# Gate and up products of three batches ahead of the norm's second half, and the down product in seven passes over all chunks

## The chip, the cores and the metric

One core of a Trainium2 chip runs the whole program. The metric is the device time of one execution in microseconds (us), lower is better. Matmuls run on TensorE (PE), elementwise work on VectorE (DVE), ScalarE (ACT) and GpSimd (POOL), and SyncE (SP) issues the DMAs. `sf`, `sr`, `hf`, `hr` are SBUF tiles, `bk` are PSUM banks, `xd`, `yd`, `td` are scratch arrays in DRAM.

## The reference

Two layers over x of 1024 tokens by 1024 features, in float32. The mixer (attention) of either layer is untouched by the change but for its first projection.

```python
for layer in range(2):
    h = rms_norm(x, attn_norm_g[layer])
    x = x + mixer(h)                      # layer 0: even_mixer, layer 1: diff_mixer
    h = rms_norm(x, ffn_norm_g[layer])
    x = x + swiglu(h, w_gate, w_up, w_down)

def swiglu(h, w_gate, w_up, w_down):      # w_gate, w_up: 1024 x 2816, w_down: 2816 x 1024
    a = einsum('bsd,df->bsf', h, w_gate)
    u = einsum('bsd,df->bsf', h, w_up)
    return einsum('bsf,fd->bsd', silu(a) * u, w_down)
```

## The kernel before, in words

Activations lie transposed: features on the 128 partitions, tokens along the free axis, in two token halves `th` = 0 and 1 of 512. Every float32 operand of a product is split in a rounded high part, which ACT casts (L102), and a low part, which DVE subtracts (L1031); a product is then three matmuls: high by high, high by low, low by high. In the gate these are L1138, L1139 and L1140, in the down product L1051, L1052 and L1053, in the output projection L374, L375 and L376.

The feed-forward multiplies by a scheme of seven products for a 2 by 2 block matrix (in place of eight), with sums of blocks made ahead of the products and sums of results behind them. In **gate and up** the left operands are the blocks of w_gate and w_up, loaded for one batch (two column tiles of 128, of eleven such pairs) at a time; the right operands B0 to B6 are the four blocks of the normalised x (rows: halves of the features; columns: halves of the tokens) and three sums of them. Only B0 and B1 are plain blocks of the first token half. One batch is seven products `i` of 2 x 4 x 3 = 24 matmuls, so a layer has 11 x 7 x 24 = 1848. `prep_gate` makes the left operands of a product (POOL sums in `left`, L1060 to L1064, then the split), `gate` runs it and drains the PSUM banks, and `hidden` writes the seven combinations of the hidden activations that the down product wants to `td`.

`out_rest` stands ahead of that: for th = 0 and then th = 1 it ends the output projection, adds the residual (L994), writes y, sums the squares, turns the sum into 1/rms (`rms`: two matmuls with a constant `sub`, L339 and L340, and DVE and ACT steps L334 to L350), and scales each of eight tiles by gain and 1/rms on DVE (L1000). For th = 0 it splits the tiles into B0 and B1; then, with both halves there, it makes the sums for B2 to B6 on DVE and POOL (L1011 to L1020) and splits them. The products stand behind all of it, batch after batch, each batch with i = 0 to 6.

**Down** takes the eleven pairs of chunks in three groups of 4, 4 and 3. Within a group all seven products run, each over the group's pairs: seven steps of 48, 48 or 36 matmuls, 924 a layer. `w_down` is loaded once per group, the right operands are read back from `td`. After each product its four banks are drained; `add_x` then reads a tile of y (residual so far) from DRAM, adds, and writes it back, once per group, and the last group writes x (layer 0) or the output (layer 1). In layer 0 the last group also feeds the next norm: squares and the split of x into the next mixer's operands.

The order of work comes from `stages`, a list of (prepare, run, ahead): `feed_forward` prepares a gate product three steps before it runs and a down product one step before. Inside that, a scheduler sets each engine's order, and pools of tiles (`Slots`) set when a buffer comes free. In layer 0 the first half's `rms` comes three steps before the end of the list and the second half's at its end; after that the next mixer starts with `first_project` (a value projection in 256-wide matmuls, L465 to L467, then L374 to L376), whose weights `w_load` splits on ACT and POOL (L220).

The lines around which the change turns:

```python
GROUPS = [range(0, 4), range(4, 8), range(8, 11)]
DOWN = [0, 1, 2, 3, 6, 4, 5]
...
for b in range(self.BATCHES):
    for i in range(7):
        yield partial(self.prep_gate, b, i), partial(self.gate, b, i), 3
for g in range(len(self.GROUPS)):
    for s in range(7):
        yield partial(self.prep_down, g, s), partial(self.down, g, s), 3 if g == s == 0 else 1
```

Of the kernel before, what the change touches and what calls it, by code (L numbers as in the profile page):

```python
# [18 lines left out]
P = 128  # L19
D = 1024  # L20
S = 1024
KC = 8
# [94 lines left out]
class Trunk:  # L117
# [379 lines left out]
    def first_project(self, st, vs, gains):  # L497
# [5 lines left out]
        for th in range(2):  # L503
            for k in range(KC):
# [297 lines left out]
    def mixer(self, l, gains, window, window_cost, forget=None):  # L802

        st, vs = deque(), deque()
        self.first_project(st, vs, gains(0))
# [163 lines left out]
    def out_rest(self, l):  # L969


        nc = self.nc
        if 6 not in self.loaded:
            self.load_o(l, 6)
        self.sr.put(*self.oH[0:6], *self.oL[0:6])
        w = [self.w_next(), self.w_next()]
        for th in range(2):
            sl = slice(th * TH, th * TH + TH)
            for k in sorted(self.apart):
                nc.sync.dma_start(self.x_tile(k, th), self.p_dram[k][:, sl])  # L980
        Slots.join(self.sr, self.sf)
        Slots.join(self.hr, self.hf, self.raw)
        self.take_raw(0)
        acc = self.sf.get()
        g0 = G_FFN0 if l == 0 else G_FFN1
        for th in range(2):
            sl = slice(th * TH, th * TH + TH)
            for k in range(KC):
                ps = self.rF.get()
                c = slice(k * P, k * P + P)  # L990
                self.mm3(ps[:], [y[2][:, 0, c] for y in w], [y[3][:, 0, c] for y in w],
                         [r32(t[:, sl]) for t in self.oH[6:]], [r32(t[:, sl]) for t in self.oL[6:]])
                x = self.x_at(k, th)
                nc.vector.tensor_tensor(x, ps[:], x, ALU.add)  # L994
                nc.sync.dma_start(self.y_dram[k][:, sl], x)
                self.squares(acc, x, k, k < 2)
            self.rms(acc, th)
            for k in range(KC):
                x = self.x_at(k, th)
                nc.vector.scalar_tensor_tensor(x, x, self.gains[:, g0 + k:g0 + k + 1], self.rt[:, sl],  # L1000
                                               ALU.mult, ALU.mult)
                if th == 0:
                    self.B[k % 2].append(self.split(x))
            if th == 0:
                self.prep_to(2)
        for x in w:
            self.sr.put(x[0], x[1])
        self.sr.put(*self.oH[6:], *self.oL[6:])
        self.sf.put(acc)
        xs = [[self.x_at(2 * j + e, t) for e in range(2) for t in range(2)] for j in range(4)]  # L1010
        for b11, b12, b21, b22 in xs:  # L1011
            nc.vector.tensor_tensor(b11, b12, b11, ALU.subtract)
            nc.gpsimd.tensor_tensor(b12, b22, b12, ALU.subtract)
            self.B[5].append(self.split(b22))
            nc.vector.tensor_tensor(b22, b22, b11, ALU.subtract)
            self.B[2].append(self.split(b22))
            nc.gpsimd.tensor_tensor(b21, b21, b22, ALU.subtract)
        for i, place in ((3, 1), (4, 0), (6, 2)):
            for j in range(4):
                self.B[i].append(self.split(xs[j][place]))  # L1020
                if i != 4:
                    self.sf.put(self.xt[(4 if i == 3 else 0) + j])

    def split(self, x):

        t = self.sr.get()
        h, l = t[:, 0:TH], t[:, TH:2 * TH]
        if len(x.shape) == 3:
            h, l = (y.rearrange("p (j c) -> p j c", j=4) for y in (h, l))
        self.S.copy(r32(h), x)  # L1030
        self.nc.vector.tensor_tensor(r32(l), x, h, ALU.subtract)  # L1031
        return t
# [8 lines left out]


    def products(self, ps, WT, BT, c, first, last):

        nc = self.nc
        n = len(WT)
        for j in range(n):
            w, b = WT[j], BT[j]
            wh, wl = r32(w[:, c]), r32(w[:, TH + c.start:TH + c.stop])
            bh, bl = r32(b[:, 0:TH]), r32(b[:, TH:2 * TH])  # L1050
            nc.tensor.matmul(ps, wh, bh, start=first and j == 0, stop=False, skip_group_check=True)  # L1051
            nc.tensor.matmul(ps, wh, bl, start=False, stop=False, skip_group_check=True)  # L1052
            nc.tensor.matmul(ps, wl, bh, start=False, stop=j == n - 1, skip_group_check=True)  # L1053

    def left(self, i, A, tmp):

        p = self.nc.gpsimd
        a11, a12, a21, a22 = A
        if i == 2:
            p.tensor_tensor(tmp, a21, a22, ALU.add)  # L1060
            p.tensor_tensor(a21, a11, a21, ALU.subtract)
            p.tensor_tensor(a11, tmp, a11, ALU.subtract)
        if i == 5:
            p.tensor_tensor(a12, a12, a11, ALU.subtract)  # L1064
        return self.split((a11, a12, a11, a21, tmp, a12, a22)[i])


    BATCHES = NF // 2

    def take_raw(self, b):  # L1070

        self.raws[b] = []
        for f in (2 * b, 2 * b + 1):
            t = [self.sf.get(), self.sf.get()]
            for x, src in zip(t, (self.a["wg"], self.a["wu"])):
                self.nc.sync.dma_start(x[:].rearrange("p (k c) -> p k c", k=8), src[self.l, f])
            self.raws[b].append(t)

    def prep_gate(self, b, i):
        if i == 1 and b + 1 < self.BATCHES:  # L1080
            self.take_raw(b + 1)
        elif b + 1 == self.BATCHES and i in (1, 4):
            self.take_down(0, 0 if i == 1 else 2)
        out = []
        for n, (g, u) in enumerate(self.raws[b]):
            A = [x[:].rearrange("p (j e c) -> p j e c", j=4, e=2)[:, :, e, :] for x in (g, u) for e in range(2)]
            if i == 2:
                self.tmp[n] = self.hf.get()
            s1 = self.tmp[n][:].rearrange("p (j c) -> p j c", j=4) if self.tmp[n] is not None else None
            out.append(self.left(i, A, s1))  # L1090
            if i == 4:
                self.hf.put(self.tmp[n])
                self.tmp[n] = None
            if i == 6:
                self.sf.put(g, u)
        return out

    def gate(self, b, i, W):
        nc = self.nc
        for n in range(2):  # L1100
# [3 lines left out]
            self.products_gate(ps, W[n], self.B[i], i)  # L1104
            self.sr.put(W[n])
            v = self.v[n]
            if i == 0:
                v["p"], v["s"] = self.hf.get(), self.hf.get()
                self.S.copy(v["p"][:], ps)
            elif i == 1:  # L1110
                self.S.activation(v["s"][:], ps, AF.Silu)
            elif i == 2:
                v["u"] = self.hf.get()
                nc.vector.tensor_tensor(v["u"][:], ps, v["p"][:], ALU.add)
            elif i == 3:
                nc.vector.tensor_tensor(v["p"][:], ps, v["p"][:], ALU.add)
            elif i == 4:
                v["q"] = self.hf.get()
                nc.vector.tensor_tensor(v["q"][:], ps, v["p"][:], ALU.add)
            elif i == 5:  # L1120
                u = v["u"][:]
                nc.vector.tensor_tensor(u, ps, u, ALU.add)
                self.S.activation(u, u, AF.Silu)
                nc.gpsimd.tensor_tensor(u, u, v["q"][:], ALU.mult)
            else:
                nc.vector.tensor_tensor(v["p"][:], ps, v["p"][:], ALU.add)
                nc.gpsimd.tensor_tensor(v["s"][:], v["s"][:], v["p"][:], ALU.mult)
        if b == self.BATCHES - 1:
            self.sr.put(*self.B[i])
        if i == 6:  # L1130
            self.hidden(b)

    def products_gate(self, ps, w, B, i):
        nc = self.nc
        for j in range(4):
            wh, wl = (r32(w[:, o + j * P:o + j * P + P]) for o in (0, TH))
            bh, bl = r32(B[j][:, 0:TH]), r32(B[j][:, TH:2 * TH])
            nc.tensor.matmul(ps, wh, bh, start=i in (0, 2, 4, 6) and j == 0, stop=False, skip_group_check=True)  # L1138
            nc.tensor.matmul(ps, wh, bl, start=False, stop=False, skip_group_check=True)  # L1139
            nc.tensor.matmul(ps, wl, bh, start=False, stop=j == 3, skip_group_check=True)  # L1140

    def hidden(self, b):

        nc = self.nc
        x, y = self.v
# [289 lines left out]
```

## Time and profile before

| | before |
|---|---|
| median of 3 runs | 2727.14 us (2722.53 to 2727.82) |
| the profiled execution: time, span | 2726.96 us, 2725.1 us |
| PE busy | 2482.8 us, 91% of the span |
| DVE, ACT, POOL busy | 1906.0, 1287.8, 958.8 us (70%, 47%, 35%) |
| DMA | 331.64 MB, mean 122 GB/s |
| chain that ended last: PE, DVE, ACT, POOL, DMA | 65%, 15%, 5%, 5%, 5% |

The span is the time from the first to the last recorded work. The busy share is a mean over stages: layer 0's feed-forward runs from about 668 to 1392 us, layer 1's from about 2006 us to the end, and in both the gate's steady part has PE busy throughout. "PEclk" in the rows below is the granted TensorE clock of a stretch, 1.00 being the higher of its two levels (2.4 GHz) and 0.50 the lower (1.2 GHz).

### The profile page before, as it was taken

To read this page: it belongs to the slowest core of one execution; us is meant where nothing else is said; L and a number is where in the kernel's file an instruction comes from. 1 tells how busy PE (TensorE), PEld (TensorE's weight loads), DVE (VectorE), ACT (ScalarE), POOL (GpSimd) and SP (SyncE) were. 2 spreads that over 40 slices of the span, in tenths; PEclk is the share of its full clock that TensorE was granted. 3 is DMA by queue.
4 is the path that set the end of the run, shared out by engine and by line. 5 is a ranking of instruction groups with operands and counts; after the bars stand their busy time and mean duration, and the time that the engine had idled before them with its cause. 6 is when DMAs were issued, how large, how long until landed. Compare 5 with 4: busy or idle time off the path is not lost.

```text
span 2725.1 us, 35163 instructions
## 1 busy us (share of the span) xinstructions
PE 2482.8 (91%) x11896; PEld 2032.0 (75%) x11896; DVE 1906.0 (70%) x3411; ACT 1287.8 (47%) x2598; POOL 958.8 (35%) x760
## 2 busy tenths in 40 slices
PE   8898899998499999998969999998967999998997
PEld 7776778776388888777758877876745888886786
DVE  6869858987865556576756687778677555656775
ACT  5656666754433233434446576666443323333332
POOL 4112111123354444424552232223134444434643
PEclk9999999999699999999989999999988999999998
DMA  5323152463023223466533232235421322345654
GB/s 174 91 57 81 28 125 82 118 208 140 34 94 108 101 105 116 175 222 208 184 130 85 67 98 76 79 90 146 138 93 66 108 101 104 116 145 200 231 182 162
DMA packets 157488, 331.64 MB, mean 122 GB/s; under 512 B 19539, under 2 KB 25460, under 8 KB 157308
## 3 DMA queue, kind: packets, MB, share of 16 engines
q1 hardware_dynamic: 157308, 329.41, 38.2%
q8 instruction: 93, 1.52, 0.2%
q14 instruction: 87, 0.71, 0.1%
HBM read 199.27 MB, written 88.11 MB: 105 GB/s over the span
## 4 chain that ended last, share of the span: by engine, by line
PE 65%; DVE 15%; ACT 5%; POOL 5%; DMA 5%; issue 4%; SPq 1%; POOLq 0%; DVEq 0%; ACTq 0%
PE bk L1139 10%; PE bk L1138 10%; PE bk L1140 10%; PE bk L375 4%; PE bk L376 4%; PE bk L374 4%; PE bk L1051 3%; PE bk L1052 3%; PE bk L1053 3%; PE bk L687 3%; PE bk L565 3%; DVE sf L583 2%; PE bk L673 2%; ACT sf L110 1%; DVE sr L1031 1%
## 5 line engine op out<-in xcount | busy, mean ns | idle before, releaser
L102 ACT CAST sr<-sf 128x512 fp32r<-128x512 f32 (+1 forms) x690 | 409.4, 620 | 777.8 <-PE bk L1140 309.0
L1031 DVE TENSOR_TENSOR sr<-sf,sr 128x512 fp32r<-128x512 f32 x628 | 515.3, 847 | 166.4 <-ACT sr L102 165.1
L1138 PE MATMUL bk<-sr,sr 128*128 128x512 f32 x1232 | 483.7, 394 | 46.7 <-ACT sr L102 45.7
L1139 PE MATMUL bk<-sr,sr 128*128 128x512 f32 x1232 | 483.9, 393 | 45.8 <-DVE sr L1031 45.8
L1140 PE MATMUL bk<-sr,sr 128*128 128x512 f32 x1232 | 481.8, 391 | 0.0
L374 PE MATMUL bk<-sr,sr 128*128 128x512 f32 x768 | 307.0, 400 | 4.9 <-ACT sr L102 2.7
L1138 PEld LDWEIGHTS bk<-sr,sr 128*128 128x128 f32 x1232 | 233.1, 190 | 100.3 <-ACT sr L102 50.0
L375 PE MATMUL bk<-sr,sr 128*128 128x512 f32 x768 | 305.6, 398 | 2.3 <-DVE sr L928 2.3
L1139 PEld LDWEIGHTS bk<-sr,sr 128*128 128x128 f32 x1232 | 233.2, 189 | 98.3 <-DVE sr L1031 50.4
L376 PE MATMUL bk<-sr,sr 128*128 128x512 f32 x768 | 304.0, 396 | 1.2 <-POOL sr L220 1.2
L220 POOL TENSOR_TENSOR sr<-raw,sr 128x512 fp32r<-128x512 f32 (+2 forms) x140 | 189.1, 1365 | 314.8 <-ACT sr L102 181.5
L1051 PE MATMUL bk<-sr,sr 128*128 128x512 f32 x616 | 249.2, 405 | 46.3 <-ACT sf L102 30.8
L1140 PEld LDWEIGHTS bk<-sr,sr 128*128 128x128 f32 x1232 | 233.0, 189 | 48.6 <-DVE sr L1031 0.4
L1052 PE MATMUL bk<-sr,sr 128*128 128x512 f32 x616 | 246.9, 401 | 0.0
L1053 PE MATMUL bk<-sr,sr 128*128 128x512 f32 x616 | 246.2, 400 | 0.0
L565 PE MATMUL bk<-sr,sr 128*128 128x512 f32 (+2 forms) x768 | 200.3, 359 | 9.0 <-ACT sf L110 8.1
L1252 POOL TENSOR_TENSOR hf<-hf,hf 128x512 f32<-128x512 f32 x72 | 106.3, 1485 | 257.5 <-DVE hf L1236 245.7
L687 PE MATMUL bk<-hr,sr 128*128 128x512 f32 (+2 forms) x560 | 165.4, 388 | 14.1 <-DVE hr L705 11.5
L1051 PEld LDWEIGHTS bk<-sr,sr 128*128 128x128 f32 x616 | 120.1, 195 | 77.6 <-ACT sf L102 35.0
L102 ACT CAST hr<-bk 128x512 fp32r<-128x512 f32 (+2 forms) x240 | 122.4, 525 | 104.8 <-PE bk L673 92.3
L705 DVE TENSOR_TENSOR hr<-bk,hr 128x512 fp32r<-128x512 f32 (+2 forms) x240 | 142.4, 604 | 41.4 <-ACT hr L102 39.9
L374 PEld LDWEIGHTS bk<-sr,sr 128*128 128x128 f32 x768 | 145.3, 189 | 33.9 <-ACT sr L102 3.7
(189 smaller groups left out, 4886.3 us busy)
## 6 DMA issues: line engine op xcount, KB each, us to landing
td<-hf SPq DMA_DIRECT2D x154, 256.0 KB, 2.0
sf<-td SPq DMA_DIRECT2D x154, 256.0 KB, 4.2
sr<-sr SPq DMA_DIRECT2D x96, 256.0 KB, 3.5
hf<-yd SPq DMA_DIRECT2D x96, 256.0 KB, 3.9
sf<-in_wg_dram SPq DMA_DIRECT2D x44, 512.0 KB, 3.9
sf<-in_wu_dram SPq DMA_DIRECT2D x44, 512.0 KB, 3.6
sf<-in_wd_dram SPq DMA_DIRECT2D x44, 512.0 KB, 5.8
raw<-in_w_dram SPq DMA_DIRECT2D x64, 256.0 KB, 3.0
```

The lines of the kernel that those rows point to most:

```text
L102: self.last = self.e.copy(out, in_)
L374: nc.tensor.matmul(ps, WH[k], hH[k], start=first and k == 0, stop=False)
L375: nc.tensor.matmul(ps, WH[k], hL[k], start=False, stop=False)
L376: nc.tensor.matmul(ps, WL[k], hH[k], start=False, stop=last and k == n - 1)
L565: nc.tensor.matmul(b[:, 0:hi - lo], r32(Q[i // 4][:, q]), r32(KK[:, lo:hi]), start=j == 0, stop=j == 1)
L1031: self.nc.vector.tensor_tensor(r32(l), x, h, ALU.subtract)
L1051: nc.tensor.matmul(ps, wh, bh, start=first and j == 0, stop=False, skip_group_check=True)
L1052: nc.tensor.matmul(ps, wh, bl, start=False, stop=False, skip_group_check=True)
L1053: nc.tensor.matmul(ps, wl, bh, start=False, stop=j == n - 1, skip_group_check=True)
L1138: nc.tensor.matmul(ps, wh, bh, start=i in (0, 2, 4, 6) and j == 0, stop=False, skip_group_check=True)
L1139: nc.tensor.matmul(ps, wh, bl, start=False, stop=False, skip_group_check=True)
L1140: nc.tensor.matmul(ps, wl, bh, start=False, stop=j == 3, skip_group_check=True)
```

## The change

It reorders the gate and rewrites the down product; the number of matmuls stays.

- **Early products.** i = 0 and 1 of batches 0, 1 and 2 come first (`EARLY = 3`); then i = 2 to 6 of these three; then batches 3 to 10 as before. `out_rest` is called once per token half. The gain is put on by ACT (`scale`), the factor 1/rms by four 1024-wide DVE products (L998). B2 to B6 are made in five parts (`rights_late`), one beside each of the steps 2 to 6, in 1024-wide operations, and their sums run on DVE alone. The results of i = 0 and 1 of batches 1 and 2 wait in an `sf` tile; w_gate of batches 1 and 2 is loaded a second time when its turn comes.
- **Down.** Seven passes, each one product over all eleven pairs: 77 steps of 12 matmuls. Each pass keeps its sums in four PSUM banks, 0 to 3 or 4 to 7 in turn, and they are drained at its end only (`take`). w_down stays in 22 SBUF tiles, loaded as 44 blocks of 256 KB a layer; the block sums (33 and 11 a layer) are made in place on POOL ahead of the passes that want them (`sums`). y is read once for each of the 16 tiles and x written once.
- **Next norm.** In layer 0 `next_norm` is spread over the last twelve steps, four `w_load` of the next mixer come in the last five, and the `rms` of the second token half moves between the halves of `first_project`, by way of a call that `mixer` hands on.

The new lines are L1046 for the low part of a 512-wide split and L1039 for a 1024-wide one, L1102 to L1104 for the gate's matmuls, L1236 to L1238 for the down product's. The diff, cut to its core:

```diff
+    def out_rest(self, l, th, w, acc, gain):
...
+            x = self.x_at(k, th)
+            self.S.activation(x, x, AF.Copy, scale=self.gains[:, gain + k:gain + k + 1])
...
+        for t in self.xt[4 * th:4 * th + 4]:
+            y = t[:].rearrange("p (e c) -> p e c", e=2)
+            nc.vector.tensor_tensor(y, y, r, ALU.mult)
...
+    def rights_late(self):
+
+        v, x = self.nc.vector, self.xt
+        for m in range(2):
+            v.tensor_tensor(x[4 + m][:], x[6 + m][:], x[4 + m][:], ALU.subtract)
+            v.tensor_tensor(x[m][:], x[4 + m][:], x[m][:], ALU.add)
+            self.B[2].append(self.split2(x[m]))
+        yield
...
+    PASSES = [0, 6, 1, 2, 4, 3, 5]
+    BLOCKS = [0, 3, 1, 2]
...
+    def sums(self, s):
+
+        p, n = self.nc.gpsimd, self.PAIRS
+        while self.n3 < n and s >= 2 * n - 2 + self.n3 * 13 // 10:
+            a11, a21, a22 = (self.block(x, self.n3) for x in (0, 2, 3))
+            p.tensor_tensor(a22, a21, a22, ALU.add)
+            p.tensor_tensor(a21, a11, a21, ALU.subtract)
+            p.tensor_tensor(a11, a22, a11, ALU.subtract)
+            self.n3 += 1
...
+    def prep_down(self, s):
+        i, j = self.PASSES[s // self.PAIRS], s % self.PAIRS
+        self.loads(s, s)
+        self.sums(s)
+        W = self.split(self.block((0, 1, 0, 2, 3, 1, 3)[i], j))
+        pool, t = self.rights.popleft()
+        R = self.split(t[:, 0:TH])
...
+        banks = self.bank[0:4] if n % 2 == 0 else self.bank[4:8]
...
+            if j == self.PAIRS - 1:
+                self.take(i, u, ps)
...
+        if i in (0, 6, 4):
+            self.S.copy(at(i), ps)
+        elif i == 2:
+            nc.vector.tensor_tensor(at(2), ps, at(0), ALU.add)
...
+        elif i == 1:
+            t = self.x_old(u, 0)
+            nc.vector.tensor_tensor(t[:], ps, t[:], ALU.add)
...
+        elif i == 3:
+            nc.vector.tensor_tensor(at(0), ps, at(0), ALU.add)
+            for x, th in ((6, 0), (4, 1)):
+                nc.vector.tensor_tensor(at(x), at(x), at(0), ALU.add)
+                self.x_new(u + 4, th, at(x))
...
+        todo = [(b, i) for b in range(self.EARLY) for i in range(2)]
+        todo += [(b, i) for b in range(self.EARLY) for i in range(2, 7)]
+        todo += [(b, i) for b in range(self.EARLY, self.BATCHES) for i in range(7)]
...
+        self.out_rest(l, 0, w, acc, gain)
+        for t in range(4):
+            self.B[t // 2].append(self.split2(self.xt[t]))
+        prep_to(2)
+        self.take_raw(0, (1,))
+        self.out_rest(l, 1, w, acc, gain)
...
+            prep_to(m + (3 if m < 7 * self.EARLY else 4 if s < 0 else 5))
+            run(made[m])
+            made[m] = None
+            if 2 <= m < 7:
+                next(late)
+            if l == 0 and (n - 12 <= s < n - 3 or s == n - 1):
+                self.next_norm(min(s - n + 12, 9))
+                if n - 5 <= s < n - 1:
+                    self.w_load()
```

On PE, at the start of layer 0's gate, the order before goes from batch 0's second product straight to its third (banks bk_67 and bk_68, right operand B2):

```order
L1139 MATMUL bk_64<-sr_6531,sr_6551 128x512
L1140 MATMUL bk_64<-sr_6531,sr_6551 128x512
L1138 MATMUL bk_67<-sr_6712,sr_6786 128x512
L1138 MATMUL bk_68<-sr_6712,sr_6789 128x512
L1139 MATMUL bk_67<-sr_6712,sr_6786 128x512
```

In the changed kernel five high-by-high matmuls of three batches come first (bk_63 and bk_64 are batch 0, bk_65 batch 1, bk_67 and bk_68 batch 2):

```order
L1102 MATMUL bk_63<-sr_6518,sr_6534 128x512
L1102 MATMUL bk_64<-sr_6518,sr_6537 128x512
L1102 MATMUL bk_65<-sr_6518,sr_6660 128x512
L1102 MATMUL bk_67<-sr_6518,sr_6728 128x512
L1102 MATMUL bk_68<-sr_6518,sr_6731 128x512
L1103 MATMUL bk_63<-sr_6519,sr_6534 128x512
L1104 MATMUL bk_63<-sr_6518,sr_6534 128x512
```

and 34 rows on from there the reduction of the second half's `rms` (L339) stands between two matmuls of batch 0:

```order
L1102 MATMUL bk_64<-sr_6526,sr_6543 128x512
L339 MATMUL bk_69<-hr_6640,sub_134 128x512
L1103 MATMUL bk_64<-sr_6527,sr_6543 128x512
```

The third product of batch 0 (bk_69) now comes 146 rows after the first of all, behind the last matmuls of batch 2's second product on bk_68:

```order
L1103 MATMUL bk_68<-sr_6531,sr_6777 128x512
L1104 MATMUL bk_68<-sr_6530,sr_6777 128x512
L1102 MATMUL bk_69<-sr_6764,sr_6818 128x512
```

So 144 matmuls of gate and the reduction stand between the start and the first need of B2, where 48 and the reduction stood.

On DVE, in layer 0's down product, the order before mixes the drains of a product (L1252, PSUM plus y) with the low parts of the next product's operands (L1031):

```order
L1252 TENSOR_TENSOR hf_9845<-bk_63,hf_9845 128x512
L1031 TENSOR_TENSOR sr_9918<-sf_9830,sr_9918 128x512
L1031 TENSOR_TENSOR sr_9995<-sf_9328,sr_9995 128x512
L1031 TENSOR_TENSOR sr_10381<-sf_9782,sr_10381 128x512
L1031 TENSOR_TENSOR sr_9998<-sf_9921,sr_9998 128x512
L1252 TENSOR_TENSOR hf_9861<-bk_64,hf_9861 128x512
```

In the changed kernel the four drains of a whole pass (here the third, whose last step is step 32) stand together, behind the weight part of step 40 (sr_10526) and ahead of its activation part:

```order
L1046 TENSOR_TENSOR sr_10526<-sf_9586,sr_10526 128x512
L1261 TENSOR_TENSOR hf_10439<-bk_63,hf_10439 128x512
L1261 TENSOR_TENSOR hf_10446<-bk_64,hf_10446 128x512
L1261 TENSOR_TENSOR hf_10453<-bk_65,hf_10453 128x512
L1261 TENSOR_TENSOR hf_10460<-bk_66,hf_10460 128x512
L1046 TENSOR_TENSOR sr_10529<-hf_10464,sr_10529 128x512
```

So at that place the splits stand seven to eight steps ahead of the products, where they stood one longer step ahead.

At the end of layer 0 DVE comes to the next norm's sum of both halves of the squares (L334) and its low part (L337) right behind the last splits of the down product:

```order
L1046 TENSOR_TENSOR sr_11381<-hf_11301,sr_11381 128x512
L315 SCALAR_TENSOR_TENSOR sr_11204<-hf_11396,gains,sr_11196 128x512
L326 TENSOR_TENSOR sf_11191<-sf_11191,hf_11400 128x512
L334 TENSOR_TENSOR sf_11191<-sf_11191 128x512
L337 TENSOR_TENSOR hr_11427<-sf_11191,hr_11426 128x512
```

PE's L339 of the next norm waits for what comes of that row.

## Rows read from the trace of the kernel before

**Rows 1.** Page: PE's busy row; the costliest cast (count | busy, mean ns | idle before it).

```profile
PE 2482.8 (91%) x11896; PEld 2032.0 (75%) x11896; DVE 1906.0 (70%) x3411; ACT 1287.8 (47%) x2598; POOL 958.8 (35%) x760
...
L102 ACT CAST sr<-sf 128x512 fp32r<-128x512 f32 (+1 forms) x690 | 409.4, 620 | 777.8 <-PE bk L1140 309.0
```

**Rows 2.** Windows: from-to, length, busy (count) by engine, PE, PEld, DVE, ACT, POOL; PEclk, DMA, GB/s.

```profile
660.00:740.00 80.00, 34.10 (x119) 24.24 (x118) 69.70 (x84) 39.18 (x62) 36.72 (x24) 0.68 0.09 33
...
800.00:1100.00 300.00, 300.00 (x1325) 248.39 (x1325) 177.95 (x221) 94.07 (x158) 135.97 (x95) 1.00 0.29 104
1140.00:1400.00 260.00, 225.95 (x948) 182.90 (x948) 185.18 (x242) 107.17 (x186) 127.71 (x86) 0.94 0.55 186
2000.00:2080.00 80.00, 33.92 (x119) 23.96 (x119) 69.12 (x81) 34.46 (x55) 34.12 (x22) 0.72 0.08 26
...
2474.00:2725.00 251.00, 221.23 (x926) 179.75 (x924) 164.67 (x215) 84.65 (x150) 114.07 (x79) 0.93 0.58 191
```

**Rows 3.** PE's timeline at layer 0's gate: start, us, instruction, idle before and releaser.

```profile
668.54 0.39 PE L376 MATMUL bk<-sr,sr 128*128 128x512 f32 x1
675.51 1.22 PE L1138 MATMUL bk<-sr,sr 128*128 128x512 f32 x2 [6.58 <-ACT sr L102]
...
731.80 0.79 PE L1139 MATMUL bk<-sr,sr 128*128 128x512 f32 x1 [18.87 <-DVE sr L1031]
...
735.86 0.39 PE L1138 MATMUL bk<-sr,sr 128*128 128x512 f32 x1
```

**Rows 4.** DVE's timeline in the same place.

```profile
667.45 0.69 DVE L326 TENSOR_TENSOR sf<-sf,hf 128x512 f32<-128x512 f32 x1
...
669.49 1.75 DVE L326 TENSOR_TENSOR sf<-sf,hf 128x512 f32<-128x512 f32 x1
671.16 1.75 DVE L350 TENSOR_TENSOR rt<-rt,hf 128x512 f32<-128x512 f32 x1
```

**Rows 5.** 1024-wide operations elsewhere: DVE at L928, ns min/median/max; ACT's casts, mean ns.

```profile
L928 DVE TENSOR_TENSOR sr<-sf,sr x14: 1205/1218/2321, 526.6 to 1926.3; 128x1024 fp32r<-128x1024 f32 x14
```

```profile
L102 ACT CAST sr<-sf 128x1024 fp32r<-128x1024 f32 x14 | 14.6, 1048 | 6.8 <-DMA sf<-od 6.7
```

**Rows 6.** Line L1051 in either layer: count, ns min/median/max, first and last start.

```profile
L1051 PE MATMUL bk<-sr,sr x308: 387/389/796, 1141.4 to 1392.0; 128*128 128x512 f32 x154
```

```profile
L1051 PE MATMUL bk<-sr,sr x308: 387/389/796, 2474.1 to 2719.0; 128*128 128x512 f32 x154
```

**Rows 7.** PE's waits in layer 0's down product: us in total, times, longest.

```profile
PE bk L1051 <- ACT sf L102: 12.6, 4, 5.2
PE bk L339 <- ACT hr L102: 7.4, 1, 7.4
PE bk L1051 <- DVE sf L1231: 6.7, 1, 6.7
```

**Rows 8.** The same in layer 1's.

```profile
PE bk L1051 <- ACT sf L102: 18.3, 5, 4.8
```

**Rows 9.** DVE's, then POOL's timeline in layer 0's down product.

```profile
1163.35 6.10 DVE L1031 TENSOR_TENSOR sr<-sf,sr 128x512 fp32r<-128x512 f32 x10
...
1237.68 4.52 DVE L1031 TENSOR_TENSOR sr<-sf,sr 128x512 fp32r<-128x512 f32 x3 [4.33 <-ACT sr L102]
```

```profile
1238.21 1.74 POOL L1060 TENSOR_TENSOR sf<-sf,sf 128x512 f32<-128x512 f32 x1
1239.92 1.73 POOL L1252 TENSOR_TENSOR hf<-hf,hf 128x512 f32<-128x512 f32 x1
```

**Rows 10.** The start of the next mixer: a window (columns of rows 2), and PE's timeline.

```profile
1392.60:1422.20 29.60, 19.96 (x116) 17.37 (x116) 11.33 (x12) 12.79 (x22) 20.35 (x15) 0.88 0.38 127
```

```profile
1401.55 0.28 PE L465 MATMUL bk<-sr,sr 128*128 128x256 f32 x1
1401.67 0.28 PE L466 MATMUL bk<-sr,sr 128*128 128x256 f32 x1
```

**Rows 11.** Timeline of the program's end.

```profile
2720.82 1.26 POOL L1252 TENSOR_TENSOR hf<-hf,hf 128x512 f32<-128x512 f32 x1 [0.76 <-DVE hf L1236]
```

More of the change, by code (lines that the diff above doesn't have):

```diff
@@ L967, in g_out_part @@
                 yield HALF * 0.75
-    def out_rest(self, l):
+    def out_rest(self, l, th, w, acc, gain):
         nc = self.nc
[L973 to L1022, printed above, removed]
@@ L1032, in split @@
-        return t
[L1043 to L1053, printed above, removed]
@@ L1079, in prep_gate @@
[L1079 to L1083, printed above, removed]
-        out = []
-        for n, (g, u) in enumerate(self.raws[b]):
-            A = [x[:].rearrange("p (j e c) -> p j e c", j=4, e=2)[:, :, e, :] for x in (g, u) for e in range(2)]
-            if i == 2:
-                self.tmp[n] = self.hf.get()
-            s1 = self.tmp[n][:].rearrange("p (j c) -> p j c", j=4) if self.tmp[n] is not None else None
-            out.append(self.left(i, A, s1))
+        self.S.copy(r32(t[:, 0:TH]), x)
@@ L1125, in gate @@
             else:
-                nc.vector.tensor_tensor(v["p"][:], ps, v["p"][:], ALU.add)
-                nc.gpsimd.tensor_tensor(v["s"][:], v["s"][:], v["p"][:], ALU.mult)
+                nc.vector.tensor_tensor(v["p"], ps, v["p"], ALU.add)
+                nc.gpsimd.tensor_tensor(v["s"], v["s"], v["p"], ALU.mult)
         if b == self.BATCHES - 1:
-            self.sr.put(*self.B[i])
+            self.sr.put(*(x for hl in self.B[i] for x in hl))
         if i == 6:
             self.hidden(b)
[L1133 to L1140, printed above, removed]
@@ L1262, in stages @@
-    def stages(self):
-        for b in range(self.BATCHES):
-            for i in range(7):
-                yield partial(self.prep_gate, b, i), partial(self.gate, b, i), 3
-        for g in range(len(self.GROUPS)):
-            for s in range(7):
-                yield partial(self.prep_down, g, s), partial(self.down, g, s), 3 if g == s == 0 else 1
-    def prep_to(self, n):
-        while len(self.made) < min(n, len(self.todo)):
-            self.made.append(self.todo[len(self.made)][0]())
+        n, j = divmod(s, self.PAIRS)
@@ L1275, in feed_forward, with last_rms @@
+    def last_rms(self):
+        self.rms(self.acc[1], 1, True)
+        self.sf.put(self.acc[1])
     def feed_forward(self, l):
+        nc = self.nc
         self.l = l
         self.B = [[] for _ in range(7)]
-        self.raws, self.downs = {}, {}
-        self.v, self.ps, self.tmp, self.tmps = [{}, {}], [None, None], [None, None], None
-        self.todo, self.made = list(self.stages()), []
-        self.out_rest(l)
-        n = len(self.todo)
-        for i, (_, run, _) in enumerate(self.todo):
-            ahead = i + 1
-            while ahead < n and ahead - self.todo[ahead][2] <= i:
-                ahead += 1
-            self.prep_to(ahead)
-            run(self.made[i])
-            self.made[i] = None
-            if l == 0 and i == n - 3:
-                self.rms(self.acc, 0, True)
@@ new lines, in feed_forward, with prep_to @@
+        gates, n = len(todo), 7 * self.PAIRS
+        todo += [(partial(self.prep_down, x), partial(self.down, x)) for x in range(n)]
+        made = []
+        def prep_to(m):
+            while len(made) < min(m, len(todo)):
+                made.append(todo[len(made)][0]())
+        self.out_rest(l, 0, w, acc, gain)
[4 more added lines that the diff above has]
+        self.out_rest(l, 1, w, acc, gain)
@@ new lines, in feed_forward @@
+        for x in w:
+            self.sr.put(x[0], x[1])
+        self.sr.put(*self.oH[6:], *self.oL[6:])
+        self.sf.put(acc)
+        late = self.rights_late()
+        for m, (_, run) in enumerate(todo):
+            s = m - gates
+            if s < 0:
+                if s >= -5:
+                    self.loads(2 * s + 11, s + 6)
+            else:
+                self.loads(min(s + 10, n - 1), s + 7)
+            prep_to(m + (3 if m < 7 * self.EARLY else 4 if s < 0 else 5))
[7 more added lines that the diff above has]
+                    self.w_load()
```

361 lines of the change are left out of this document (223 added, 138 removed).

## The prediction

> **What bounds the kernel now.** I read the page first. TensorE is busy for 91% of the span [rows 1], so the rest is what can go while the matmuls stay: the change keeps their number. Then windows by stage. In the gate's steady part 1325 matmuls fill 300 us without a gap at the full clock [rows 2], 0.2264 us each; this is the pitch that every stage is held against. Three stages fall short of it.
>
> Gate start: 119 matmuls in the 80 us from 660 us, and as many in the 80 us from 2000 us [rows 2]. At the pitch they need 26.9 us, so **53.1 us are lost in each layer**. The timeline of PE shows where: a wait of 6.6 us behind the output projection for the first casts, and one of 18.9 us for the low parts of B2 [rows 3]. While PE waits, DVE is busy for 69.7 of 80 us: it is the bound there.
>
> Down: from the first to the last L1051 it is 250.6 us in layer 0 and 244.9 us in layer 1 [rows 6]; the 921 matmuls between need 208.5 us. With about 1 us for the norm's few matmuls in layer 0 that loses **41 and 36.4 us**. The waits there are for ACT's casts, for drains (L1231), and in layer 0 for the next norm [rows 7, 8]: each product's operands are made in one lump, one step ahead, behind the drains of the product before.
>
> Start of mixer 1: 116 matmuls in 29.6 us [rows 10]. 96 of them are 256 wide at 0.12 us (the two starts in rows 10 differ by that), which is 11.5 us, and with the rest, at their own widths, 15.1 us. **14.5 us are lost.**
>
> **Part by part.** The profiled execution took 2726.96 us, 0.2 under the median, so the sum against it stands for both.
>
> *Early products.* Between start and first need of B2 stand 144 matmuls in place of 48, which is 33 us of work in place of 11. What is left of the loss, in order:
> - Start. The projection's last matmul ends at 668.9 us [rows 3]. DVE's L326 takes 1.75 us there beside POOL, where it took 0.69 alone, and L350 ends at 672.9 [rows 4]; fewer block sums on POOL beside it should bring that to 670 to 672. Then four 1024-wide products with 1/rms and the first low part, 1.2 us each, beside the first cast of 1.05 us [rows 5], so PE goes on at about 678 us: 9 us.
> - The clock. After 18.9 us of idling a matmul takes 0.79 us and only 4 us later 0.39 again [rows 3]: 9 or 10 matmuls at double pitch, 2 us.
> - The second half's rms. L339 now stands 40 matmuls in, at 687 us. DVE has eight 1024-wide operations (9.6 us) and the sums of squares ahead of L337, which so ends near 691: 4.5 us.
> - B2. 106 matmuls later, 24 us, its low part is wanted; DVE has the rest of the rms (6 us), four products, four sums and two low parts (12 us), and some 8 splits and drains (5 us), with POOL's pair price on some of them, near 29 us in all: 5.5 us.
> - Left operands of batches 1 and 2, split beside all that: 5 us, between 0 and 10.
>
> Together 27 us in place of 53: **26 gained a layer, 52 in both.** Nearest bounds: 12 lost if only start, clock and a little of the rest stay, 42 if DVE stays as full as now (69.7 of 80 us) and each of the last three waits doubles. The gain on ACT and the second load of w_gate (two batches, 2 MB a layer) I cost at nothing: ACT is busy for 39 of 80 us and the DMA for a tenth [rows 2]; without that cover the 2 MB would take 11 us at the 186 GB/s of the down product's window [rows 2], which is inside the bounds.
>
> *Down by passes.* Twelve matmuls a step are 2.72 us. A step wants two casts, 1.24 us [rows 1], and two low parts, 1.22 us (ten took 6.10) [rows 9]. Both fit. Drains fall from 28 a group to 28 a layer, the y traffic from three readings to one. What can spoil it is DVE beside POOL: there a low part takes 1.5 us (three took 4.52) and POOL's sum 1.74, against 1.30 for POOL without it [rows 9]. Of 44 POOL sums most lie beside DVE work: 44 by 1.7 is 75 us, in which DVE makes 44 low parts, 22 steps, while PE runs 27.5. DVE falls back 5.5 steps or 15 us. The order has the splits seven to eight steps ahead (the 1.5 steps that drains take off leave 17.7 us), so the lag is just covered, in the middle at **nothing**. This is the thinnest cover of the whole sum; if it is gone the price is in the second rival. At the beginning I put 1 us. At layer 0's end DVE has 41 operations, of which ten beside POOL, from the pass's last drains to L337: 36 us against 24.4 us of PE's last nine steps, so L339 waits for 11 us where 7.4 stood [rows 7]. Layer 0 keeps 12 of 41: **29 gained** (bounds 4 to 20 kept). Layer 1 has no next norm and keeps 3 of 36.4: **33 gained** (1 to 10 kept).
>
> *A rule that speaks against it.* The row shows a pair of one DVE low part and one POOL sum at about 1.7 us [rows 9]. The Trainium skill, SBUF — State Buffer, "SBUF: two separate sides", says that VectorE with two SBUF inputs and GpSimd share one port pair as an exclusive lock, held for the whole instruction while the other blocks fully. By that a pair would cost the sum of both, 0.61 and 1.30, 1.91 us; 44 of them would make a lag of 24 us, 6.5 us over the lead, and the whole would come to 2614 us. The measured pair decides, so I keep 1.7.
>
> *Mixer 1's start.* POOL's L220 and the casts are done before, in the last five steps, and the second rms hides behind half of the projection: 3 of 14.5 us stay (1 to 8), **11 gained**. What is late next is that same rms; its cover is 48 narrow matmuls, 5.8 us, and L1265 to L337 of the end above has been paid already.
>
> *End.* The last matmul starts two behind the last L1051 and ends at 2719.8 us; then a PSUM drain, a POOL addition of 1.26 us that ends at 2722.1, and the write to the end of the span at 2725.1 [rows 6, 11]. The POOL addition is no longer there: **1.3 gained**.
>
> Sum: 52 + 29 + 33 + 11 + 1.3 = 126.3; 2727.0 less that is **2601 us**. All bounds together give 2558 to 2650.
>
> **Rivals.**
> 1. *The gate start keeps its stalls.* DVE is the bound there, and its work does not shrink (wide operations save some fixed time, B2's sums come over from POOL). If the third product is as late as before and the early ones only fill it in part, 42 us are lost, 11 gained a layer: 2631. For: DVE's 69.7 of 80 us. Against: 22 us more of matmuls ahead of B2.
> 2. *DVE and POOL use up the lead in the down product.* Waits at each step of passes 3 to 7: 15 us a layer more, and 8 at layer 0's end: 2639. For: the lag of 15 us against 17.7 rests on one row. Against: splits may have run further ahead by then. With the first rival: 2669.
> 3. *Slower: the splits stop running ahead.* Operand tiles and landing buffers are pools; if their slots come free only with the release of PE's last matmul of a step, a step is serial: 2.72 + 1.24 + 0.61 = 4.57 us, 77 of them 352 us in place of 251 and 246. With the other gains of 64 us that is 2871. It decides from a mean step of 3.65 us (154 such steps use up those 64 us and the 497 us of both layers now). For: w_down now holds 22 tiles of the same pool. Against: the order shows the splits ahead.
> 4. *The change does not do what it says*: the early products stand in PE's order, but their left operands come no earlier than B2. Then the time stays within a few us of 2727.
>
> **How the numbers follow.** Forecast 0.58; first rival 0.17, second 0.13, both 0.04; third 0.05; fourth 0.03, of which 0.02 within 0.2% (5.5 us, about what a measurement of this kernel can tell from no change) and 0.01 slower. Faster is 0.58 + 0.17 + 0.13 + 0.04 = 0.92, slower 0.06. The range goes from the lower bound of the sum, 2558, to 2665: it holds the first two rivals with some spread and nearly both together, and leaves out the third and fourth and the edges.
>
> **What would show it.** Right: 119 matmuls from the end of the projection in about 54 us rather than 80; no wait over 3 us for B2's low part beside others; L1236 to L1238 dense from the third pass on, with waits below 5 us a layer save for L339; the mixer's first 116 matmuls in 18 us. Wrong in the second rival's way: PE's L1236 or L1237 waits for DVE L1046 a microsecond or so at a time while POOL is in `sums`. Wrong in the third's: such a wait at each of the 77 steps. Should the clock fall to the lower level in the down product, these numbers don't hold.

## The result, and the profile after

The changed kernel takes **2613.64 us** (median of four, 2613.05 to 2617.48), against 2727.38 before: ratio 0.959, interval 0.9573 to 0.9606. The forecast was 2601, its range 2558 to 2665. The profiled execution, the slowest of the four (2617.48 us), has a span of 2615.7 us, 109.4 less than before.

Cut at matmuls that both traces have (the projection's last ahead of the gate, the down product's first and last), the spans are:

| stretch | before, us | after, us | gained | forecast |
|---|---|---|---|---|
| gate, layer 0 and 1 | 472.9, 473.6 | 459.1, 461.5 | 13.8, 12.1 | 26, 26 |
| down, layer 0 and 1 | 250.6, 244.9 | 220.5, 208.8 | 30.1, 36.1 | 29, 33 |
| mixer 1, to its projection's last matmul | 608.5 | 591.5 | 17.0 | 11 |
| last L1051 or L1236 to the end | 6.1 | 4.6 | 1.5 | 1.3 |

These gains sum to 110.6 us; mixer 0, which the change leaves alone, is 1.2 longer in this execution. Down and mixer gave more than forecast, the gate half. The windows of after, in the columns of [rows 2]:

```profile
660.00:740.00 80.00, 64.01 (x264) 50.57 (x263) 68.63 (x69) 52.11 (x76) 20.84 (x12) 0.89 0.13 45
740.00:800.00 60.00, 50.09 (x206) 39.78 (x206) 35.46 (x46) 14.51 (x25) 34.78 (x24) 0.94 0.36 128
800.00:840.00 40.00, 37.21 (x164) 30.48 (x163) 23.92 (x29) 12.16 (x23) 24.95 (x18) 1.00 0.36 126
...
2402.00:2611.00 209.00, 209.00 (x924) 173.06 (x923) 157.98 (x164) 83.13 (x148) 93.72 (x58) 1.00 0.45 143
```

264 matmuls stand in the first 80 us where 119 stood. But the 60 us behind, which hold 265 in the steady part, hold 206: a loss of 13 us. In the 40 us after that 164 stand for 177, 3 us more. The kernel before lost nothing in the same place:

```profile
740.00:800.00 60.00, 60.00 (x266) 49.71 (x265) 35.45 (x46) 18.07 (x30) 26.71 (x20) 1.00 0.28 101
```

Layer 1's down product is dense: 924 matmuls in 209 us. Its waits of [rows 8] are gone; in layer 0, of [rows 7], the list of PE's waits has left:

```profile
PE bk L339 <- ACT hr L102: 7.6, 1, 7.6
PE bk L1237 <- DVE sr L1046: 0.6, 1, 0.6
```

PE's timeline of the gate's start (compare [rows 3]): rows with a wait, and at 721.55 us the 145th matmul of the gate, the first that wants B2:

```profile
678.01 2.50 PE L1102 MATMUL bk<-sr,sr 128*128 128x512 f32 x5 [7.89 <-ACT sr L102]
685.79 0.79 PE L1103 MATMUL bk<-sr,sr 128*128 128x512 f32 x1 [5.28 <-DVE sr L1039]
...
705.77 0.50 PE L1102 MATMUL bk<-sr,sr 128*128 128x512 f32 x1 [1.07 <-ACT sf L102]
...
721.55 0.39 PE L1102 MATMUL bk<-sr,sr 128*128 128x512 f32 x1
...
729.72 0.50 PE L1104 MATMUL bk<-sr,sr 128*128 128x512 f32 x1 [1.67 <-DVE sr L1046]
...
763.12 0.80 PE L1102 MATMUL bk<-sr,sr 128*128 128x512 f32 x1 [6.80 <-DVE hf L1123]
```

The wait for B2's operands, 18.9 us before, is gone: PE comes to B2 without a wait. Two small waits stand near it, and neither is for B2: 1.07 us at batch 1's second product, for a PSUM bank that ACT drains late, and 1.67 us for the low part of a left operand, of batch 0's fifth product, which PE starts ahead of the fourth. In front PE waits 13.2 us in place of the 9 forecast, and further on there is a new wait of 6.8. Why the front is late stands in DVE's timeline, and POOL's beside it:

```profile
674.60 8.93 DVE L998 TENSOR_TENSOR sf<-sf,rt 128x1024 f32<-128x1024 f32 x4
683.45 6.72 DVE L1039 TENSOR_TENSOR sr<-sf,sr 128x1024 fp32r<-128x1024 f32 x3
```

```profile
680.20 2.25 POOL L1074 TENSOR_TENSOR sf<-sf,sf 128x512 f32<-128x512 f32 x1
682.41 2.25 POOL L1077 TENSOR_TENSOR sf<-sf 128x512 f32<-128x512 f32 x1
```

The wide operations take 2.24 us each, not the 1.2 of [rows 5]: POOL sums batch 0's blocks meanwhile.

Both small waits go back to ACT's timeline, in the second half's rms:

```profile
696.43 1.28 ACT L110 ACT_TABLE_LOAD   x1
697.73 0.63 ACT L110 ACTIVATE hf<-hf 128x512 f32<-128x512 f32 x1
698.38 1.28 ACT L110 ACT_TABLE_LOAD   x1
699.67 0.69 ACT L110 ACTIVATE rt<-bk,eps 128x512 f32<-128x512 f32 x1
...
700.86 1.28 ACT L110 ACT_TABLE_LOAD   x1
702.15 0.63 ACT L110 ACTIVATE rt<-rt 128x512 f32<-128x512 f32 x1
702.80 1.28 ACT L110 ACT_TABLE_LOAD   x1
704.10 0.63 ACT L110 ACTIVATE hf<-hf 128x512 f32<-128x512 f32 x1
...
705.15 1.05 ACT L102 COPY sf<-bk 128x512 f32<-128x512 f32 x2
```

Batch 0's two Silu (hf<-hf) stand between L339 and the end of the rms; each pulls the tables away from Ln (rt<-bk) and Exp (rt<-rt). Four loads and two Silu are 6.4 us ahead of the drain (sf<-bk) that the first small wait is for, and on a chain that DVE waits for (DVE's timeline):

```profile
705.28 0.69 DVE L348 SCALAR_TENSOR_TENSOR hf<-bk,hf 128x512 f32<-128x512 f32 x1 [8.62 <-ACT hf L110]
...
716.28 4.63 DVE L1039 TENSOR_TENSOR sr<-sf,sr 128x1024 fp32r<-128x1024 f32 x4
...
728.99 1.28 DVE L1046 TENSOR_TENSOR sr<-hf,sr 128x512 fp32r<-128x512 f32 x2
```

B2's low parts are among the four L1039, which end by 720.9 us, before PE wants them. The last row has the low part of the second small wait.

### The profile page after: what moved, and what is told of

Same layout as the page of the kernel before. It is cut to its first block, busy times and chain, and to the rows that moved or that the text cites. A ratio compares the mean times of both kernels' runs of the same rounds, so it can differ in the third digit from the quotient of the medians.

```text
span 2615.7 us, 34768 instructions
## 1 busy us (share of the span) xinstructions
PE 2464.4 (94%) x11896; PEld 2018.6 (77%) x11896; DVE 1893.3 (72%) x3271; ACT 1301.6 (50%) x2616; POOL 886.1 (34%) x696
## 4 chain that ended last, share of the span: by engine, by line
PE 67%; DVE 15%; ACT 6%; POOL 4%; issue 4%; DMA 3%; SPq 0%; POOLq 0%; DVEq 0%; ACTq 0%
PE bk L1102 8%; PE bk L1104 8%; PE bk L1103 8%; PE bk L1237 5%; PE bk L1238 5%; PE bk L1236 5%; PE bk L375 4%; PE bk L376 4%; PE bk L374 4%; PE bk L689 4%; PE bk L567 3%; DVE sf L585 3%; PE bk L675 2%; ACT sf L110 2%; PE bk L466 1%
## 5 line engine op out<-in xcount | busy, mean ns | idle before, releaser
L102 ACT CAST sr<-sf 128x512 fp32r<-128x512 f32 (+2 forms) x516 | 320.7, 642 | 566.5 <-PE bk L1104 191.8
L1102 PE MATMUL bk<-sr,sr 128*128 128x512 f32 x1232 | 487.8, 398 | 43.8 <-ACT sr L102 15.8
L1046 DVE TENSOR_TENSOR sr<-sf,sr 128x512 fp32r<-128x512 f32 x426 | 397.2, 938 | 129.5 <-ACT sr L102 127.4
L1104 PE MATMUL bk<-sr,sr 128*128 128x512 f32 x1232 | 483.1, 393 | 3.3 <-DVE sr L1046 3.3
L1102 PEld LDWEIGHTS bk<-sr,sr 128*128 128x128 f32 x1232 | 235.1, 191 | 104.3 <-DVE hf L1123 21.6
L374 PE MATMUL bk<-sr,sr 128*128 128x512 f32 x768 | 306.7, 400 | 5.5 <-DVE hf L427 3.0
L1103 PEld LDWEIGHTS bk<-sr,sr 128*128 128x128 f32 x1232 | 234.4, 190 | 60.2 <-DVE sr L1039 12.0
L1104 PEld LDWEIGHTS bk<-sr,sr 128*128 128x128 f32 x1232 | 234.1, 190 | 53.4 <-DVE sr L1046 4.2
L1236 PE MATMUL bk<-sr,sr 128*128 128x512 f32 x616 | 240.4, 390 | 0.0
L1238 PE MATMUL bk<-sr,sr 128*128 128x512 f32 x616 | 240.2, 390 | 0.0
L102 ACT CAST sr<-hf 128x512 fp32r<-128x512 f32 (+1 forms) x260 | 161.2, 620 | 139.5 <-DMA hf<-td 71.8
L1046 DVE TENSOR_TENSOR sr<-hf,sr 128x512 fp32r<-128x512 f32 x190 | 194.8, 1033 | 27.3 <-ACT sr L102 26.7
L374 PEld LDWEIGHTS bk<-sr,sr 128*128 128x128 f32 x768 | 145.1, 189 | 34.4 <-DVE hf L427 3.7
```

Source lines behind the costliest of these rows:

```text
L102: self.last = self.e.copy(out, in_)
L374: nc.tensor.matmul(ps, WH[k], hH[k], start=first and k == 0, stop=False)
L1046: self.nc.vector.tensor_tensor(r32(t[:, TH:2 * TH]), x, t[:, 0:TH], ALU.subtract)
L1236: nc.tensor.matmul(ps, wh, bh, start=i in (0, 6, 2, 4) and j == 0, stop=False, skip_group_check=True)
L1238: nc.tensor.matmul(ps, wl, bh, start=False, stop=j == self.PAIRS - 1, skip_group_check=True)
```

## The experiments

Three questions: what the early products are worth, what holds the gate now, and what the down product's density rests on. All are edits of the changed kernel, compared with the kernel before on the same chip (2723.9 to 2725.2 us there). The intervals are about 0.0013 of the time to either side, 3.5 us, so a difference of a few us between two edits is not clear of noise.

**early1 and early2: fewer batches ahead.**

```diff
-    EARLY = 3
+    EARLY = 1
...
-            if 2 <= m < 7:
+            if m < 5:
```

> Only batch 0's first two products stand ahead of the third (as in the kernel before); all else as changed. If the early products work by covering the wait for B2 (A): 96 matmuls less ahead of B2 make that wait 96 x 0.2264 = 21.7 us longer in each layer (1.7 us to about 23), and some 2 us of lower clock behind it; the wait of 6.8 us for the drain of batch 1's third product, with its clock and the small ones after it some 14 us, goes, since batch 1's first two products stand in between again. Net 10 us a layer slower than the changed kernel: about 2634 us. If the early products cost nothing (B): the 13 us a layer that the gate gained are lost and more, 22 a layer: 2658. If they are worth nothing and the gate's gain came from the wide operations (C): 2614.

> Two batches early in place of three. (A) 48 matmuls less ahead of B2: 10.9 us a layer more wait there, one boundary without cover (batch 0 to 1) in place of two: the stall of 6.8 us and its clock stay, the small waits behind (about 5 us) go. Net 5 us a layer slower: about 2624. (B) 22 us slower in all: 2636. (C) 2614.

`early1` took 2633.46 us (0.9665, 0.9652 to 0.9678), as A says: PE waits 17.8 us for B2's casts and 1.1 for its low part, and the early products are worth 20 of the 114 us (18 of the 26 in the gate, whose spans are 469.0 and 470.0 us). The expectation starts from a wait of 1.7 us for B2 in the changed kernel; there is none, and B2 is some 3 us early, so 19 was to be expected, which is what stands. `early2` (which only sets `EARLY = 2`) took 2631.25 (0.9658, 0.9644 to 0.9671), not 2624: the wait for B2 is 5.3 and 1.1 us, but the wait for the drain of batch 1's third product is 9.1 us, not 6.8. The third batch gives 18 us, the second 2, which is within the intervals.

**pool_late, silu_late, early1_silu and start_three: the start.** `pool_late` makes POOL's first sum depend on B1's last low part; `silu_late` orders the Silu behind the rms; `start_three` has both, and issues L339 behind the first two products (there L342).

```diff
+                if b == 0:
+                    p.tensor_copy(s1[:, 0:1], self.B[1][1][1][:, 0:1])
```

```diff
         self.S.activation(t[:], r, AF.Square)
+        self.rms_last = self.S.last
...
-                    self.S.activation(v["s"], v["s"], AF.Silu)
+                    with self.tc.issue_after(self.rms_last.ins):
+                        self.S.activation(v["s"], v["s"], AF.Silu)
```

> POOL's block sums of batch 0 wait until B1's last low part is made. If DVE's four scalings and first low parts take 2.24 us each, in place of 1.2, because POOL sums run beside them: seven of them at 1.2 let PE's first L1103 start 5 us earlier in each layer: about 2604. If the price only moves to the second half's scalings and B2's operands, where POOL then runs: L1103 early, but the wait for B2 grows by as much: 2614.

`pool_late` took 2613.77 us (0.9595, 0.9581 to 0.9608): no gain, the second expectation. PE's timeline has the first low part early and the gain given back to L339 and the clock (0.79 us a matmul behind each wait):

```profile
677.91 0.79 PE L1105 MATMUL bk<-sr,sr 128*128 128x512 f32 x1 [0.97 <-DVE sr L1039]
692.15 0.79 PE L339 MATMUL bk<-hr,sub 128*128 128x512 f32 x1 [3.69 <-ACT hr L102]
694.90 0.80 PE L340 MATMUL bk<-hr,sub 128*128 128x512 f32 x1 [0.67 <-DVE hr L337]
```

It moved from the operands to the rms, not, as expected, to B2, for which PE does not wait here either. Behind L339 DVE is busy for only 10.5 of 20 us and idles 9.4 us for ACT, so ACT's chain, and not DVE's work, sets when B2 is made.

> The two Silu of batch 0 are put behind the second rms on ACT; in the changed kernel they stand within it, and four table loads of 1.28 us with them. If the chain from L339 over ACT's Ln and Exp to DVE's scaling bounds B2: it gets some 6 us shorter, and the waits of PE for it (1.7 and 1.1 us a layer) go; no more can be gained, since PE's own 146 matmuls end 2.7 us before B2 now: about 2608. If DVE's work bounds B2, not ACT's chain: the waits stay, 2614.

> The same with only batch 0 early, where PE waits 17.8 us for B2 and the whole of the shorter chain shows: 6.4 us a layer less than with one batch early and the Silu within (2633): about 2621. If ACT's table loads are not on the path: 2633.

`silu_late` took 2607.88 us (0.9569, 0.9556 to 0.9582), `early1_silu` 2619.92 (0.9615, 0.9602 to 0.9628): both as the first theory in time. In `silu_late` both small waits are gone, though neither was for B2 as its expectation has it; the gates are 3.8 and 6.2 us shorter, with a new wait of 2.3 and 2.5 us for a drain at batch 0's sixth product. In `early1_silu`, where PE does wait for B2, that wait falls from 17.8 to 11.6 us. ACT's timeline of `silu_late` has no load left within the rms:

```profile
694.42 0.69 ACT L110 ACTIVATE rt<-bk,eps 128x512 f32<-128x512 f32 x1 [0.83 <-PE bk L340]
695.14 0.63 ACT L110 ACTIVATE rt<-rt 128x512 f32<-128x512 f32 x1
695.80 0.63 ACT L110 ACTIVATE hf<-rt 128x512 f32<-128x512 f32 x1
696.45 1.28 ACT L110 ACT_TABLE_LOAD   x1
```

The Trainium skill, ScalarE: Activation LUTs, "Table sets: the hidden batching unit", asks for activations to be batched by set; these runs agree, at 13.5 us for one batch early.

> Three edits at the start of the gate: POOL's sums of batch 0 behind B1's last low part, batch 0's Silu behind the second rms, and that rms's first matmul (L339) behind the first two products in PE's order, 51 matmuls in, no longer 40. If ACT's chain and not DVE bounds B2, the 6 us that the late sums gave at the first low part are no longer given back: B2 is ready 54 to 55 us behind the projection's end, in place of 60, and the gate's start is 5.5 us a layer shorter: about 2602. If the contention only moves, no more than the 2.7 us a layer of the Silu alone: 2608.

`start_three` took 2600.32 us (0.9542, 0.9529 to 0.9555). Late sums alone gave nothing; with the Silu out of the chain and L339 further back they do: PE waits 7.3 us at the front, where 13.2 stood, and 2.2 us for the rms, and the gates are 6.2 and 7.7 us shorter than in the changed kernel. Which of the two lets them pay was not tried apart. DVE's timeline of `start_three` has four scalings in 5.7 us and four low parts in 4.6:

```profile
674.37 5.69 DVE L1007 TENSOR_TENSOR sf<-sf,rt 128x1024 f32<-128x1024 f32 x4
679.98 4.62 DVE L1048 TENSOR_TENSOR sr<-sf,sr 128x1024 fp32r<-128x1024 f32 x4
```

**hidden_late, hidden0_late and four_edits: the batch boundary.** After batch 0's seventh product comes batch 1's third, whose drain (L1123) stands on DVE behind batch 0's combinations (L1151 to L1154), which wait for POOL (DVE's timeline of the changed kernel):

```profile
755.73 1.75 DVE L1153 TENSOR_TENSOR hf<-hf,hf 128x512 f32<-128x512 f32 x1 [0.59 <-POOL hf L1136]
...
761.77 0.69 DVE L1154 TENSOR_TENSOR hf<-hf,hf 128x512 f32<-128x512 f32 x1 [1.15 <-POOL hf L1139]
762.38 0.68 DVE L1123 TENSOR_TENSOR hf<-bk,sf 128x512 f32<-128x512 f32 x1
```

Before, 48 matmuls of the next batch's first two products stood there. `hidden_late`:

```diff
-        if i == 6:
+        if i == 6 and b + 1 >= self.EARLY:
             self.hidden(b)
+        if i == 2 and 0 < b < self.EARLY:
+            with self.tc.issue_after(self.after_u.ins):
+                self.hidden(b - 1)
```

`self.after_u` is the drain L1123. `hidden0_late` does it for b = 0 alone.

> The four combinations of batch 0's and batch 1's hidden activations are put behind the drains of the next batch's third product in DVE's order. If PE's 6.8 us wait at the boundary comes of DVE's order (L1151 to L1154 wait for POOL ahead of L1123): the wait shrinks to about 1.5 us, the clock does not fall there, 8 us a layer are gained: about 2598. If the drain waits for a free tile or for POOL's port and not for that order: 2614, with a wait of 6 us or more at the same place.

> Only batch 0's combinations go behind the drains of batch 1's third product; batch 1's stay where they were. If the 6.1 us wait at the end of batch 2 that came with both late is due to tiles that batch 1 gives back later, it is 2.8 us again and 8 us a layer are gained: about 2598. If it is due to POOL, which stands before batch 3's block sums and is reached earlier by PE: the wait stays near 6 us, and the time near 2610.

`hidden_late` took 2610.32 us (0.9586, 0.957 to 0.9602): the wait is 2.2 us, so DVE's order was its cause, but 6.1 us stand behind batch 2's end where 2.8 stood, and the time is within the intervals of the changed kernel's. `hidden0_late` took 2608.15 (0.9567, 0.9554 to 0.958), with 4.4 us there in layer 0, between its two expectations, and 3.0 in layer 1, where 2.9 stood; 3.2 and 3.4 us stand at batch 1's sixth product, where 1.7 and 1.8 did. What makes these later waits is not settled: tiles and POOL's order can both do it.

> The three of start_three and batch 0's combinations behind batch 1's drains (hidden0_late, which gained 1.0 us in layer 0's gate and 5.4 in layer 1's). If they are independent: 5 us less than start_three, about 2597. If the tiles given back later take it again: as start_three, 2602.

`four_edits` took **2590.87 us** (0.9507, 0.9494 to 0.952), the fastest here: 22.8 us under the changed kernel, where its parts gave 13.3 and 5.5. Beside `start_three` the gates are 5.4 and 4.9 us shorter. In its layer 0, PE's timeline has these waits behind the rms:

```profile
750.47 0.50 PE L1113 MATMUL bk<-sr,sr 128*128 128x512 f32 x1 [1.76 <-DVE hf L1135]
766.97 0.56 PE L1113 MATMUL bk<-sr,sr 128*128 128x512 f32 x1 [2.60 <-DVE hf L1144]
786.21 0.47 PE L1113 MATMUL bk<-sr,sr 128*128 128x512 f32 x1 [0.60 <-DVE hf L1135]
813.87 0.50 PE L1113 MATMUL bk<-sr,sr 128*128 128x512 f32 x1 [2.94 <-ACT hf L102]
```

**sums_on_dve and sums_twice: the down product's cover.** `sums_on_dve` sets `p = self.nc.vector` in `sums`; `sums_twice` runs each sum into a spare tile first.

> The 44 sums run on DVE in place of POOL. By the pair price, a sum that costs DVE 0.61 us itself cost it 1.70 - 0.61 = 1.09 us beside POOL: the lead falls less, to 10 us or more at step 33. PE is dense in both, so the time stays: 2614, within 4 us. If DVE's own load was the bound (44 x 0.61 = 27 us more), PE waits there and the time rises by 5 us a layer or more: over 2624.

> Each of the 44 block sums on POOL in the down product is computed twice, the first time into a spare tile; the result is unchanged. In the changed kernel the low parts end 24 us before their matmuls at step 0 and 2.5 to 4 us before at step 33. If DVE beside POOL at 1.70 us a pair sets that fall: 44 more pairs at 1.70 against the 1.36 us a low part may take are 15 us of lag, less the 3 us left: 12 us lost a layer, 24 in all: about 2638, and PE waits for L1046 at each step from about step 33 on. If the lead runs on other things: within 5 us of 2614.

`sums_on_dve` took 2615.88 us (0.9598, 0.9584 to 0.9611): no change. The later of a step's two low parts ends 15 to 20 us ahead of its matmuls from step 15 to step 33; in the changed kernel that lead falls from 17 to 4 us in layer 0 and from 15 to 3 in layer 1. So the sums on POOL made the lag, at the pair price, as both timelines of the changed kernel show, with starts 1.70 us apart (DVE, then POOL):

```profile
1186.04 1.78 DVE L1046 TENSOR_TENSOR sr<-sf,sr 128x512 fp32r<-128x512 f32 x1
1187.74 1.78 DVE L1046 TENSOR_TENSOR sr<-hf,sr 128x512 fp32r<-128x512 f32 x1
```

```profile
1185.65 1.62 POOL L1196 TENSOR_TENSOR sf<-sf 128x512 f32<-128x512 f32 x1
1187.35 1.62 POOL L1197 TENSOR_TENSOR sf<-sf,sf 128x512 f32<-128x512 f32 x1
```

`sums_twice` took 2672.53 us (0.9805, 0.9792 to 0.9819), far over both expectations. The lead falls no faster up to step 30 (POOL was already busy throughout); then PE waits once for 20.5 us in layer 0 and 21.0 in layer 1, beside 6.0 and 0.9 us for L1046, for an ACT cast that waits for a read from `td` (ACT's timeline of `sums_twice`):

```profile
1230.06 0.62 ACT L102 CAST sr<-hf 128x512 fp32r<-128x512 f32 x1 [31.25 <-DMA hf<-td]
```

That read wants a tile of the pool that the residual tiles (and here the spare one) come from, and POOL's additions that free them stand behind the sums. This was not tried apart. It does show that the doubled sums, with their spare tile, cost more than DVE's pace explains.

**rms_late: layer 0's end.** The next norm's first `rms` moves from step n == 8 of `next_norm` behind the last one.

> In layer 0 the next norm's first reduction (L339 and what follows) is issued behind the last step of the down product, no longer nine steps before. If PE's 7.6 us wait at L339 comes only of where it stands (DVE reaches L337 late and PE, in order, stands before 90 matmuls that are ready): the wait and some 2 us of lower clock go, 9 to 10 us: about 2604. If DVE's work up to it is the bound, the same wait turns up in the next mixer's first projection, whose drains want the result: 2614.

It took 2613.23 us (0.9585, 0.9572 to 0.9598), no gain: the down product is 10.8 us shorter and mixer 1 is 9.6 longer. Its matmuls now stand there, with waits of 4.4 us around them (0.40, 0.48, 0.65 and 2.86); by the first L374 mixer 1 is 8.5 of the 9.6 us later, and the granted clock of its first 31 us is 0.94 where it was 1.00. The time is that of the second expectation (the work up to the rms is the bound, not its place), though the waits that turn up are smaller than the 7.6 us that went.

## Why the prediction was right, and where it was not

- **Early products: 52 forecast, 25.9 measured.** The failed step is a term that the sum puts at nothing: what PE waits for behind the early batches. The forecast's own terms (they add up to 26 us, not the 27 of the text) came to 20 us in the window up to 740 us. The front was mis-sized: "1.2 us each" was 2.24 beside POOL, so the first low part came at 685.8, not 678, and PE waited 13.2 us for 9. The later waits were over-priced: L339 cost none for 4.5, B2 none for 5.5, the left operands 1.7 for 5; a late drain, 1.1, has no term. The 13 us of the window from 740 us and the 3 us behind it stand in no term. At the end of batch 0 the first two products that used to cover the combinations are gone. The text asked what is late next for a stall that goes; for the two products that move away from each boundary it did not ask. `hidden_late` shows this for the wait of 6.8 us; the smaller waits there were not tried apart.
- **Down: 62 forecast, 66 measured.** On both layers the splits ran ahead and the waits of [rows 7, 8] went, save that at L339, as forecast. No run takes the passes back, so how much of the 66 us comes from the lead and how much from fewer drains and readings of y is not shown. The lead was 15 to 17 us when the sums set in, where 17.7 stood; the sums took 12 of it, and 15 beside `sums_on_dve`, where 15 stood; 2 to 4 us were left. The pair costs 1.70 us, as taken; the 1.30 us of a POOL sum alone is in the trace of before, but not in [rows 9]. By the lock rule of the Trainium skill (SBUF — State Buffer, "SBUF: two separate sides") it would be the sum of both, 1.91. At that price a wait of some 6.5 us would stand in each layer; PE waits 0.6 us for L1046 in layer 0 and not at all in layer 1, so here the rule overstates the price a little. The 2614 us that the prediction gives by that rule is the measured time by chance: its extra 13 us were to be lost in the down product, which gained more than forecast.
- **Layer 0's end: 11 us at L339 forecast, 7.6 measured**, and it stays, as said.
- **Mixer 1: 11 forecast, 17.0 measured.** Its first 31 us have no idle PE at all; the 3 us kept for the second rms were hidden. 17.0 is more than the 14.5 us lost at that start, and where the rest comes from is not shown. Mixer 0, which no run changes, has its last projection matmul at 665.9 to 671.1 us in these traces, so a few us can be scatter.
- **The total.** That 2614 us lies in the range is partly luck: the gate gave 26 us less than forecast, down and mixer 1 together 10 more.
- **Rivals.** The first (start keeps its stalls, 11 gained a layer) describes the gate's 12 to 14 best, though by another mechanism: the stalls at B2 did go. The second and third did not come: the splits ran ahead.

## What to carry to other kernels

Work that is pulled ahead leaves a place without cover: go to that place too, and ask which drains stood behind the work that left. A chain is only as short as its order on every engine: look in the order of the changed kernel for functions of another table set, and for operations of POOL beside wide DVE ones, within the chain that the change shortens. One edit that gives nothing may be the one that pays when the next chain is cut, as the late sums did together with two others.

## What the runs showed of the hardware

- A 1024-wide DVE operation on two SBUF operands took 2.24 us beside POOL's sums and 1.16 without (`start_three`); POOL's 512-wide sum took 2.25 there, where its addition alone took 1.26 [rows 11]. So both slow down, to nearly the sum of the two, 2.42.
- Ln, then a copy, then Exp cost a table load of 1.28 us each once a Silu had been between; with the set that the first rms loads still in place neither loads (`silu_late`).
- After a wait of 3.7 us (`pool_late`) and one of 2.7 (`silu_late`) the next matmul took 0.79 us, at the lower level; after one of 2.9 us (`four_edits`) and one of 4.1 (`silu_late`) it took 0.50, and the granted clock fell to 0.50 about 1 us later. So here the length of a wait alone does not tell when the clock falls.
